# Large GpSimd operations of a two-layer hybrid decoder trunk move to VectorE and ScalarE

## The chip, the cores and the metric

The kernel runs on one core of a Trainium2 chip. The metric is the device time of one execution in microseconds: 1724.83 us, the median of 3 runs (1724.72 to 1726.2). The core has TensorE (matrix products, with a separate path that loads weights), VectorE, ScalarE and GpSimd (elementwise work and reductions), and SyncE, which issues the DMA transfers of this kernel. Each engine works through its own instructions in the order in which they were written out, and waits on semaphores for those of others.

## The reference

Sequence 512, width 1024, batch 1, two layers, all in float32. Each layer has three sub-layers with a pre-RMSNorm and a residual add:

```python
for l in range(DEPTH):
    h = rms_norm(x, norm_mix[l])
    p_a, p_b, p_c, p_d = jnp.split(h @ w_in[l], splits, axis=-1)
    y = jnp.concatenate([rglru_group(p_a, ...), retention_group(p_b, ...),
                         rwkv7_group(p_c, ...), ssd_group(p_d, ...)], axis=-1)
    x = x + y @ w_out[l]
    x = x + memory_cross_attention(rms_norm(x, norm_mem_q[l]), rms_norm(mem, norm_mem_kv[l]), ...)
    x = x + swiglu(rms_norm(x, norm_ffn[l]), ffn_w_in[l], ffn_w_out[l])
return rms_norm(x, norm_final)
```

The four mixer groups are 256 wide each. RG-LRU is a gated linear recurrence behind a causal convolution. Retention is decay attention in chunks of 128, followed by a norm over each head of 64 and a SiLU gate. RWKV-7 is a recurrence with a rank-one correction per step, followed by a head norm, a bonus term and a gate. The Mamba-2 SSD group is decay attention in chunks, followed by a gate and a group norm. Cross-attention has 4 heads over 256 memory tokens, and the FFN is 2816 wide.

## The kernel before

Activations lie transposed, as tiles of 128 channels by 512 tokens (kind `s`). Large products are taken in three parts for precision: a float32 operand is split into a high part, which ScalarE rounds to fp32r by a cast, and a low part, the source minus the high part, which is a subtraction. `mm3` (line 623) then runs high x high, high x low and low x high. `split_to` (line 600) splits activations. `weights` (line 608) loads a 128-column strip of a weight matrix by DMA into a tile `u`, casts it to a tile `v` on ScalarE and writes the low part, 128x1024, to a tile `w`. There are three tiles of each kind. `project` (line 633) multiplies all 8 tiles of the normalised input by such a strip into an accumulator of kind `a`.

The order of all instructions is not written by hand. Every call such as `V.tensor_tensor(...)` is recorded (`record`, line 291) with a modelled duration (`cost`, line 365: by engine and by elements, each engine by itself), and `order` (line 402) plans the whole program as a list: at each step it takes the operation that can start first, with a class and the longest path behind it as tie-breakers, and gives it its buffers. Weight loads have a class of their own that comes first at equal start, and dense projections keep their order among themselves and fill what is left. What the plan fixes is the order on each engine. Actual times come from the chip.

A layer runs as follows (`mix`, line 1317). `normed` (line 712) sums the squares of the 8 tiles, takes the reciprocal root in small steps on VectorE (`rsqrt`, line 561), and for each tile scales it by gain and norm and splits it. TensorE is given the projection of the memory tokens to K (`MemKV.k`, line 1604) to work on meanwhile. In layer 0 `mem_stats` (line 1362) sums the squares of the memory tokens. Then come the RWKV-7 projections and `rwkv_pair`, and `rwkv_solve` (line 1163), which inverts unit triangular 32x32 blocks on GpSimd in 62 small dependent operations, two per step, with a round trip through DRAM scratch on either side. Meanwhile TensorE has the projections of the SSD group, retention and RG-LRU. `rwkv_scan` (line 1233), `ssd` (line 814), `retention` (line 987) and `lru` (line 916) follow, then the head norms (`head_norm`, line 971) and the gates with their own projections, and at the end of the mixer V of the memory (`MemKV.v`, line 1630). The output projection, cross-attention and FFN come after.

Before the change GpSimd had, besides the solve:

- the low parts of the memory's K weights (layer 0: the strips 5 to 7 of 8; layer 1: all 8), of the gates' projections (`late`, line 1350: seven strips in each layer) and of the first half of the memory's V weights (four in each layer): 33 in all
- the low parts of every second tile in `normed`
- both elementwise passes of retention's head norm on each of its two tiles
- the products in `lru` (four in each layer), `lru_gate` and `ret_gate` (two each), and the additions of the state term in `ssd` (two in each of three chunks)
- the squares of the memory tokens and their sum in `mem_stats`
- the clearing of 16 tiles of 128x512 in `rwkv_solve` and `rwkv_scan`, beside that of the solve's own tile

Of the kernel before, what the change touches and what calls it, by code (L numbers as in the profile page):

```python
# [10 lines left out]
F32 = mybir.dt.float32  # L11
# [7 lines left out]
T = 512  # L19
L = 2  # L20
P = 128
# [496 lines left out]
class Trunk:  # L518
# [74 lines left out]

    def split(self, src, scale=None, n=T, eng=None):

        hi, lo = self.S(F32R), self.S(F32R)
        self.split_to(hi[:, :n], lo[:, :n], src, scale, eng)
        return hi, lo

    def split_to(self, hi, lo, src, scale=None, eng=None):  # L600
        if scale is None:
            self.A.copy(hi, src)
            (eng or self.V).tensor_tensor(lo, src, hi.bitcast(F32), op=ALU.subtract)
        else:
            self.A.activation(hi, src, AF.Copy, scale=scale)
            self.V.scalar_tensor_tensor(lo, src, scale, hi.bitcast(F32), op0=ALU.mult, op1=ALU.subtract)

    def weights(self, src, kt, cols, eng=None, parts=1, between=lambda: None):

        r, h, lo = [self.s.tile(k, dt)[:, :kt * cols].rearrange("p (k c) -> p k c", k=kt)  # L610
                    for k, dt in (("u", F32), ("v", F32R), ("w", F32R))]
        with self.s.mode(0, "w"):
            n = kt // parts
            for i in range(parts):
                ks = slice(i * n, (i + 1) * n)
                self.Q.dma_start(r[:, ks], src[i * n * P:(i + 1) * n * P].rearrange("(k p) c -> p k c", p=P))
                if i == 0:
                    between()
                self.A.copy(h[:, ks], r[:, ks])
                (eng or self.V).tensor_tensor(lo[:, ks], r[:, ks], h[:, ks].bitcast(F32), op=ALU.subtract)  # L620
        return h, lo
# [10 lines left out]

    def project(self, w_dram, c0, xs, eng=None):

        nk = len(xs)
        out = self.acc()
        for u0 in range(0, nk, 8):
            kt = min(8, nk - u0)
            h, lo = self.weights(w_dram[u0 * P:(u0 + kt) * P, c0:c0 + P], kt, P, eng)
# [72 lines left out]
    def normed(self, xs, gain):  # L712

        _, rb = self.rms(xs)
        hat = []
        for j, x in enumerate(xs):
            y = self.S()
            self.V.scalar_tensor_tensor(y, x, gain(j), rb, op0=ALU.mult, op1=ALU.mult)
            hat.append(self.split(y, eng=self.G if j % 2 else None))
        return hat  # L720
# [93 lines left out]
    def ssd(self, l, proj, dtcum):  # L814
# [11 lines left out]
        for j in range(4):  # L826
# [50 lines left out]
            for g in range(2):  # L877
                V.scalar_tensor_tensor(yy[g][:, tk], xs[g][:, tk], self.d["dh", l][:, g:g + 1], yb[:, g * P:(g + 1) * P],
                                       op0=ALU.mult, op1=ALU.add)
                if j:  # L880
                    G.tensor_tensor(yy[g][:, tk], yy[g][:, tk], yi[:, g], op=ALU.add)
            if j < 3:
# [33 lines left out]
    def lru(self, l, proj):  # L916
# [6 lines left out]
        for i in range(2):  # L923
# [22 lines left out]
            V.scalar_tensor_tensor(ti, ti, 1.0, xc, op0=ALU.add, op1=ALU.mult)  # L946
            G.tensor_tensor(ti, ti, rc, op=ALU.mult)
            res.append((a, ti, t))
        for y, (a, ti, t) in zip(yy, res):

            self.s.link(last, A.activation(t, t, AF.Sqrt), True)
            G.tensor_tensor(ti, ti, t, op=ALU.mult)
            V.tensor_tensor_scan(y, a, ti, 0.0, op0=ALU.mult, op1=ALU.add)
        return yy

    def lru_gate(self, l, proj, yy):
        V, A = self.V, self.A
        res = []
        for i in range(2):
# [6 lines left out]
            V.scalar_tensor_tensor(q, q, 1.0, x, op0=ALU.add, op1=ALU.mult)  # L966
            self.G.tensor_tensor(yy[i], q, yy[i], op=ALU.mult)
            res.append((yy[i], 0.5))
        return res

    def head_norm(self, y, eps, eng):

# [6 lines left out]
        V.tensor_scalar(m[:, :n], m[:, :n], 1.0 / HD, None, op0=ALU.mult)  # L979
        eng.tensor_tensor(y3, y3, over(m), op=ALU.subtract)  # L980
        sq = self.S()
        A.activation(sq, y, AF.Square)
        V.tensor_reduce(m[:, n:], sq.rearrange("p (g c) -> p g c", c=HD), axis=AX.X, op=ALU.add)
        V.tensor_scalar(m[:, n:], m[:, n:], 1.0 / HD, eps, op0=ALU.mult, op1=ALU.add)
        eng.tensor_tensor(y3, y3, over(self.rsqrt(m[:, n:], n)), op=ALU.mult)

    def retention(self, l, proj, vals):
# [62 lines left out]
        for t in yt:  # L1050
            self.head_norm(t, 1e-5, G)
        yy = []
# [8 lines left out]
    def ret_gate(self, l, proj, yy):  # L1061
        res = []
        for i in range(2):
            g = self.two_silu(proj(COL_B + 768 + i * P))
            self.G.tensor_tensor(yy[i], yy[i], g, op=ALU.mult)
            res.append((yy[i], 0.5))
        return res
# [95 lines left out]
    def rwkv_solve(self, l, nd):  # L1163


        A, G = self.A, self.G
        B, H = 32, 16
# [23 lines left out]
        for k, f in enumerate((rt, rf)):  # L1191
# [4 lines left out]
            for i in range(2):  # L1196
                t = self.S()
                self.s.link(done, G.memset(t, 0.0), False)
                t3 = t.rearrange("p (n x) -> p n x", n=8)
# [33 lines left out]
    def rwkv_scan(self, l, pairs, RT):  # L1233


        V, A, E, G = self.V, self.A, self.E, self.G
        ident = self.con("ident")
# [55 lines left out]
        for i in range(2):  # L1293
            y = yt[i]
            self.head_norm(y, HD * 1e-5, V)
            b = self.bank()
# [20 lines left out]
    def mix(self, l, xs, kv):  # L1317
# [30 lines left out]
        with part("lru"):  # L1348
            ya = self.lru(l, proj)
        late = lambda c0: self.project(w, c0, hat, self.G)  # L1350
        with part("rwkv_gate"):
            rc = self.rwkv_gate(l, lora, late, yc)
        with part("ssd"):
            rd = self.ssd_gate(l, late, yd)
        with part("ret"):
            rb = self.ret_gate(l, late, yb)
        with part("lru"):
            ra = self.lru_gate(l, late, ya)
        kv.v(0)
        return ra + rb + rc + rd  # L1360

    def mem_stats(self, xs):

        V, A, E, G = self.V, self.A, self.E, self.G
# [206 lines left out]
class MemKV:  # L1571


    def weights(self, d, **k):
        tr = self.tr
        early = self.l == 0
        return tr.weights(tr.a["mem_wk"][self.l][:, d * P:(d + 1) * P], KD, P, tr.V if early and d in (0, 1, 2, 3, 4) else tr.G,
                          2 if early and d < 3 else 1, **k)

# [50 lines left out]
    def v(self, dh):  # L1630
# [36 lines left out]
```

## Time and profile before

| | |
|---|---|
| median of 3 runs | 1724.83 us (1724.72 to 1726.2) |
| the profiled execution: its own time | 1725.3 us |
| the profiled execution: span from first to last instruction | 1723.5 us |
| TensorE products | 96% of the span |
| VectorE | 1017.1 us, 59% |
| ScalarE | 631.1 us, 37% |
| GpSimd | 220.1 us, 13% |
| mean granted clock of TensorE | 0.985 of full speed |

Nearly all instructions carry one line of the source, 515, where the planned order is issued. So groups are told apart by tile names: `a` and `b` are accumulators, `s` activations, `t` small columns, `u`, `v`, `w` weights with their high and low parts, `n` the solve's matrix, `cst` and `prm` constants and parameters. In the rows PE is TensorE, DVE VectorE, ACT ScalarE, POOL GpSimd and SP SyncE. `fp32r` after a form marks a high or a low part. A group's mean is in nanoseconds, and all else is in microseconds from the first instruction.

### The profile page before, as it was taken

What the parts mean: (1) busy time and instruction counts of PE and PEld (TensorE: products, weight loads), DVE (VectorE), ACT (ScalarE), POOL (GpSimd) and SP (SyncE); (2) the same over time, 40 slices, a digit from 0 to 9 for tenths busy, and PEclk for the clock granted to TensorE, in tenths of its full rate; (3) what the DMA queues carried; (4) which work ended last, traced back from release to release, by engine and by line L of the source; (5) the groups of instructions that cost most, each with busy time, mean ns of one, the idle gap of its engine ahead of it and who ended that gap; (6) DMA issues with size and microseconds to landing.
All of it is one profiled execution on the core that took longest, in us unless ns stands there. A gap on an engine that the chain in (4) does not pass through costs nothing.

```text
span 1723.5 us, 21453 instructions
## 1 busy us (share of the span) xinstructions
PE 1662.0 (96%) x8344; PEld 1354.3 (79%) x8344; DVE 1017.1 (59%) x1700; ACT 631.1 (37%) x962; POOL 220.1 (13%) x240
## 2 busy tenths in 40 slices
PE   7898998999999999999989989999999999999997
PEld 6686776888788888888887867778887888888886
DVE  7766668675665554432467656876665645554323
ACT  6434234444442332222345333454443422332221
POOL 2316025300000000000050421351000000000001
PEclk9998999999999999999999999999999999999999
DMA  7434121441333333333453341116322333233331
GB/s 232 124 100 109 39 55 52 150 141 55 92 98 97 89 96 98 95 98 106 142 163 87 99 92 52 47 61 190 92 79 88 91 98 98 87 97 92 95 95 62
DMA packets 312901, 169.49 MB, mean 98 GB/s; under 512 B 35936, under 2 KB 300384, under 8 KB 312672
## 3 DMA queue, kind: packets, MB, share of 16 engines
q1 hardware_dynamic: 312800, 168.12, 34.1%
q8 instruction: 66, 1.08, 0.3%
q14 instruction: 35, 0.29, 0.1%
HBM read 156.56 MB, written 9.44 MB: 96 GB/s over the span
## 4 chain that ended last, share of the span: by engine, by line
PE 82%; DVE 6%; POOL 3%; ACT 1%; issue 1%; DMA 1%; SPq 1%; DVEq 0%; POOLq 0%; ACTq 0%
PE a L515 73%; PE b L515 10%; DVE s L515 4%; DVE t L515 2%; POOL s L515 2%; POOL n L515 2%; ACT s L515 1%; SPq L515 1%; ACT v L515 0%; DVE w L515 0%; DMA s<-fd 0%; DMA n<-nd 0%; DMA s<-in_lora_dram 0%; DMA nd<-s 0%; DVEq L1663 0%
## 5 line engine op out<-in xcount | busy, mean ns | idle before, releaser
L515 PE MATMUL a<-s,v 128*128 128x512 f32 (+1 forms) x4012 | 1242.5, 389 | 14.5 <-ACT s L515 8.9
L515 PEld LDWEIGHTS a<-s,v 128*128 128x128 f32 x4012 | 748.9, 190 | 174.5 <-ACT s L515 9.7
L515 PE MATMUL a<-s,w 128*128 128x512 f32 (+1 forms) x2006 | 781.9, 390 | 2.8 <-POOL w L515 1.7
L515 ACT CAST v<-u 128x1024 fp32r<-128x1024 f32 (+3 forms) x275 | 282.2, 1027 | 681.1 <-PE a L515 380.7
L515 PEld LDWEIGHTS a<-s,w 128*128 128x128 f32 x2006 | 381.5, 190 | 83.7 <-POOL w L515 1.9
L515 DVE TENSOR_TENSOR w<-u,v 128x1024 fp32r<-128x1024 f32 (+3 forms) x242 | 293.1, 1212 | 154.3 <-ACT v L515 150.9
L515 DVE TENSOR_TENSOR s<-a,s 128x512 f32<-128x512 f32 (+1 forms) x132 | 90.7, 691 | 260.9 <-PE a L515 242.2
L515 ACT ACTIVATE s<-s 128x512 f32<-128x512 f32 (+3 forms) x229 | 142.1, 628 | 123.9 <-DVE s L515 110.1
L515 PE MATMUL b<-s,s 128*64 128x64 f32 (+8 forms) x1268 | 151.3, 273 | 17.3 <-DVE s L515 6.1
L515 POOL TENSOR_TENSOR w<-u,v 128x1024 fp32r<-128x1024 f32 x33 | 82.6, 2507 | 640.7 <-ACT v L515 609.1
L515 PEld LDWEIGHTS b<-s,s 128*128 128x128 f32 (+3 forms) x1268 | 122.1, 167 | 53.0 <-issue 16.0
L515 DVE TENSOR_TENSOR s<-s,s 128x512 f32<-128x512 f32 (+3 forms) x184 | 133.8, 733 | 27.4 <-ACT s L515 21.4
L515 POOL TENSOR_TENSOR s<-s,s 128x512 f32<-128x512 f32 (+3 forms) x45 | 54.7, 1229 | 688.3 <-ACT s L515 561.4
L515 DVE SCALAR_TENSOR_TENSOR s<-s,s 128x512 f32<-128x512 f32 (+2 forms) x164 | 115.9, 711 | 23.4 <-ACT s L515 22.8
L515 DVE TENSOR_TENSOR s<-s,a 128x512 f32<-128x512 f32 (+1 forms) x49 | 33.2, 677 | 100.9 <-PE a L515 100.9
L515 DVE SCALAR_TENSOR_TENSOR s<-s,prm,s 128x512 fp32r<-128x512 f32 (+3 forms) x78 | 63.1, 833 | 8.8 <-ACT s L515 8.5
L515 PE MATMUL a<-v,s 128*128 128x260 f32 (+1 forms) x256 | 66.7, 343 | 0.0
L515 ACT COPY s<-b 64x256 f32<-64x256 f32 (+3 forms) x92 | 30.5, 353 | 98.2 <-PE b L515 96.5
L515 PE MATMUL b<-cst,s 128*128 128x128 f32 (+2 forms) x312 | 52.4, 281 | 6.8 <-POOL s L515 3.2
L515 PEld LDWEIGHTS b<-cst,s 128*128 128x128 f32 x312 | 41.7, 172 | 15.4 <-POOL s L515 4.1
L515 ACT CAST s<-s 128x512 fp32r<-128x512 f32 x48 | 29.5, 620 | 62.1 <-DVE s L515 57.0
L515 DVE SCALAR_TENSOR_TENSOR s<-a,prm,s 128x511 f32<-128x511 f32 (+2 forms) x64 | 47.6, 744 | 2.0 <-ACT s L515 1.2
(94 smaller groups left out, 788.5 us busy)
## 6 DMA issues: line engine op xcount, KB each, us to landing
u<-in_ffn_w_in_dram SPq DMA_DIRECT2D x88, 512.0 KB, 3.7
u<-in_w_in_dram SPq DMA_DIRECT2D x52, 512.0 KB, 3.8
u<-in_ffn_w_out_dram SPq DMA_DIRECT2D x32, 512.0 KB, 3.7
u<-in_mem_wv_dram SPq DMA_DIRECT2D x16, 512.0 KB, 3.6
u<-in_w_out_dram SPq DMA_DIRECT2D x16, 512.0 KB, 3.9
u<-in_mem_wq_dram SPq DMA_DIRECT2D x16, 512.0 KB, 3.8
u<-in_mem_wo_dram SPq DMA_DIRECT2D x16, 512.0 KB, 3.7
u<-in_mem_wk_dram SPq DMA_DIRECT2D x13, 512.0 KB, 3.8
```

Of the source, the lines that this page charges most:

```text
L515: op.fn(*[real(x) for x in op.args], **{k: real(x) for k, x in op.kw.items()})
```

## The change

All of the operations listed above leave GpSimd. The squares of `mem_stats` go to ScalarE, the rest to VectorE. GpSimd keeps the solve with the clearing of its own tile, and three scalings in `finish` (line 1522), each taken in two halves. The parameters that named an engine go. Nothing else is edited, but the plan is worked out again from the new list, so the order on every engine may differ. The core of the diff:

```diff
-    def split_to(self, hi, lo, src, scale=None, eng=None):
+    def split_to(self, hi, lo, src, scale=None):
-            (eng or self.V).tensor_tensor(lo, src, hi.bitcast(F32), op=ALU.subtract)
+            self.V.tensor_tensor(lo, src, hi.bitcast(F32), op=ALU.subtract)
...
-                (eng or self.V).tensor_tensor(lo[:, ks], r[:, ks], h[:, ks].bitcast(F32), op=ALU.subtract)
+                self.V.tensor_tensor(lo[:, ks], r[:, ks], h[:, ks].bitcast(F32), op=ALU.subtract)
...
-            hat.append(self.split(y, eng=self.G if j % 2 else None))
+            hat.append(self.split(y))
...
-                    G.tensor_tensor(yy[g][:, tk], yy[g][:, tk], yi[:, g], op=ALU.add)
+                    V.tensor_tensor(yy[g][:, tk], yy[g][:, tk], yi[:, g], op=ALU.add)
...
-            G.tensor_tensor(ti, ti, rc, op=ALU.mult)
+            V.tensor_tensor(ti, ti, rc, op=ALU.mult)
...
-            G.tensor_tensor(ti, ti, t, op=ALU.mult)
+            V.tensor_tensor(ti, ti, t, op=ALU.mult)
...
-        eng.tensor_tensor(y3, y3, over(m), op=ALU.subtract)
+        V.tensor_tensor(y3, y3, over(m), op=ALU.subtract)
...
-        eng.tensor_tensor(y3, y3, over(self.rsqrt(m[:, n:], n)), op=ALU.mult)
+        V.tensor_tensor(y3, y3, over(self.rsqrt(m[:, n:], n)), op=ALU.mult)
...
-                self.s.link(done, G.memset(t, 0.0), False)
+                self.s.link(done, V.memset(t, 0.0), False)
...
-                self.s.link(self.solved, G.memset(t, 0.0), False)
+                self.s.link(self.solved, V.memset(t, 0.0), False)
...
-        late = lambda c0: self.project(w, c0, hat, self.G)
-            rc = self.rwkv_gate(l, lora, late, yc)
+            rc = self.rwkv_gate(l, lora, proj, yc)
...
-            self.s.link(self.s.anchor, G.tensor_tensor(sq, m, m, op=ALU.mult), False)
+            self.s.link(self.s.anchor, A.activation(sq, m, AF.Square), False)
...
-                G.tensor_tensor(s, s, sq, op=ALU.add)
+                V.tensor_tensor(s, s, sq, op=ALU.add)
...
-            h, wl = tr.weights(tr.a["mem_wv"][self.l][u * 256:(u + 1) * 256, dh * T:(dh + 1) * T], 2, T, None if dh else tr.G)
+            h, wl = tr.weights(tr.a["mem_wv"][self.l][u * 256:(u + 1) * 256, dh * T:(dh + 1) * T], 2, T)
```

In this order the edits are in `split_to`, `weights`, `normed`, `ssd`, `lru` (two), `head_norm` (two), `rwkv_solve`, `rwkv_scan`, `mix`, `mem_stats` (two) and `MemKV.v`. `MemKV.weights` loses its choice of engine in the same way, and the three other gates are called with `proj` too. One product each in `lru_gate` and `ret_gate` moves likewise. `link(a, b, False)` puts `b` behind `a` in the plan. It adds no semaphore of its own.

## Rows read from the trace of the kernel before

**Rows 1.** The page: busy time by engine (1), one costly group (5).

```profile
PE 1662.0 (96%) x8344; PEld 1354.3 (79%) x8344; DVE 1017.1 (59%) x1700; ACT 631.1 (37%) x962; POOL 220.1 (13%) x240
...
L515 ACT ACTIVATE s<-s 128x512 f32<-128x512 f32 (+3 forms) x229 | 142.1, 628 | 123.9 <-DVE s L515 110.1
```

**Rows 2.** Busy time by stretch: span, each engine (x instructions), PEclk, DMA share, GB/s.

```profile
23.00:62.00 39.00, 28.87 (x156) 23.94 (x157) 32.89 (x32) 15.75 (x24) 26.32 (x17) 0.87 0.57 171
246.00:288.00 42.00, 34.74 (x169) 27.11 (x170) 38.21 (x99) 20.90 (x31) 19.16 (x11) 0.94 0.12 38
866.00:899.00 33.00, 27.44 (x208) 26.40 (x207) 27.35 (x28) 16.08 (x27) 23.17 (x13) 0.95 0.54 158
155.00:172.00 17.00, 11.08 (x67) 8.57 (x66) 8.69 (x17) 8.97 (x18) 4.22 (x11) 0.70 0.64 122
```

**Rows 3.** TensorE's timeline: start, length, instruction, [idle before, what ended it].

```profile
49.97 0.50 PE L515 MATMUL a<-s,v 128*128 128x512 f32 x1 [4.05 <-DVE s L515]
...
273.16 0.66 PE L515 MATMUL b<-cst,s 128*128 128x128 f32 x4 [1.58 <-POOL s L515]
...
282.24 0.82 PE L515 MATMUL b<-s,s 128*128 128x512 f32 x2 [2.88 <-DVE s L515]
```

**Rows 4.** Timeline of GpSimd and VectorE, lengths in us.

```profile
256.50 3.03 POOL L515 TENSOR_TENSOR w<-u,v 128x1024 fp32r<-128x1024 f32 x1 [5.18 <-ACT v L515]
...
257.18 2.38 DVE L515 TENSOR_SCALAR t<-t 128x8 f32<-128x8 f32 x1
...
887.99 0.68 DVE L515 TENSOR_TENSOR s<-s,s 128x512 fp32r<-128x512 f32 x1
```

**Rows 5.** VectorE by form, 866 to 899 us: count, busy us, mean ns, idle.

```profile
L515 DVE SCALAR_TENSOR_TENSOR s<-s,prm,s 128x512 f32<-128x512 f32 x8 | 11.2, 1453 | 1.6 <-ACT s L515 1.6
...
L515 DVE TENSOR_TENSOR s<-s,s 128x512 fp32r<-128x512 f32 x4 | 6.4, 1598 | 1.2 <-ACT s L515 1.2
...
L515 DVE TENSOR_TENSOR w<-u,v 128x1024 fp32r<-128x1024 f32 x2 | 4.5, 2294 | 0.0
...
L515 DVE TENSOR_TENSOR s<-s,s 128x512 f32<-128x512 f32 x1 | 2.5, 2509 | 0.7 <-ACT s L515 0.7
...
L515 DVE SCALAR_TENSOR_TENSOR t<-t,t 128x4 f32<-128x4 f32 x6 | 1.0, 164 | 0.2
```

**Rows 6.** VectorE by form, 23 to 62 us.

```profile
L515 DVE SCALAR_TENSOR_TENSOR s<-s,prm,s 128x512 f32<-128x512 f32 x8 | 10.6, 1366 | 1.8 <-ACT s L515 1.8
...
L515 DVE TENSOR_TENSOR s<-s,s 128x512 fp32r<-128x512 f32 x6 | 9.0, 1508 | 1.4 <-ACT s L515 1.4
...
L515 DVE SCALAR_TENSOR_TENSOR t<-t,t 128x4 f32<-128x4 f32 x6 | 3.1, 524 | 0.2
...
L515 DVE TENSOR_SCALAR t<-t 128x4 int32<-128x4 int32 x2 | 2.3, 1166 | 0.1
```

**Rows 7.** VectorE by form, 62 to 121 us.

```profile
L515 DVE TENSOR_TENSOR w<-u,v 128x1024 fp32r<-128x1024 f32 x5 | 6.1, 1226 | 3.3 <-ACT v L515 2.9 <-issue 0.2
...
L515 DVE SCALAR_TENSOR_TENSOR s<-s,prm,s 128x512 f32<-128x512 f32 x2 | 1.5, 752 | 0.1
```

**Rows 8.** VectorE by form, 246 to 288 us.

```profile
L515 DVE SCALAR_TENSOR_TENSOR t<-t,t 128x8 f32<-128x8 f32 x24 | 8.1, 366 | 0.1
...
L515 DVE TENSOR_SCALAR t<-t 128x8 f32<-128x8 f32 x7 | 4.1, 600 | 0.0
...
L515 DVE TENSOR_TENSOR s<-s,s 128x512 f32<-128x512 f32 x2 | 2.4, 1208 | 2.8 <-ACT s L515 2.8
```

**Rows 9.** GpSimd by form, 246 to 288 us.

```profile
L515 POOL TENSOR_TENSOR w<-u,v 128x1024 fp32r<-128x1024 f32 x3 | 7.8, 2606 | 7.7 <-ACT v L515 5.2 <-PE b L515 2.5
...
L515 POOL TENSOR_TENSOR s<-s,t 128x512 f32<-128x512 f32 x4 | 5.3, 1314 | 13.7 <-DVE t L515 13.7
```

**Rows 10.** Chain of waits, 304 to 376 us: start, length, what.

```profile
304.77 70.10 PE a L515 x302
```

**Rows 11.** VectorE's waits by releaser: us in total, times, longest us.

```profile
DVE w L515 <- ACT v L515: 150.9, 141, 4.8
```

More of the change, by code (lines that the diff above doesn't have):

```diff
@@ L592, in softplus, with split @@
         V.scalar_tensor_tensor(out, h, 2.0, s, op0=ALU.mult, op1=ALU.add)
-    def split(self, src, scale=None, n=T, eng=None):
+    def split(self, src, scale=None, n=T):
         hi, lo = self.S(F32R), self.S(F32R)
-        self.split_to(hi[:, :n], lo[:, :n], src, scale, eng)
+        self.split_to(hi[:, :n], lo[:, :n], src, scale)
         return hi, lo
-    def split_to(self, hi, lo, src, scale=None, eng=None):
+    def split_to(self, hi, lo, src, scale=None):
         if scale is None:
             self.A.copy(hi, src)
-            (eng or self.V).tensor_tensor(lo, src, hi.bitcast(F32), op=ALU.subtract)
+            self.V.tensor_tensor(lo, src, hi.bitcast(F32), op=ALU.subtract)
         else:
@@ L606, in split_to, with weights @@
             self.V.scalar_tensor_tensor(lo, src, scale, hi.bitcast(F32), op0=ALU.mult, op1=ALU.subtract)
-    def weights(self, src, kt, cols, eng=None, parts=1, between=lambda: None):
+    def weights(self, src, kt, cols, parts=1, between=lambda: None):
         r, h, lo = [self.s.tile(k, dt)[:, :kt * cols].rearrange("p (k c) -> p k c", k=kt)
@@ L631, in dense, with project @@
         return self.s.mode(2, "d")
-    def project(self, w_dram, c0, xs, eng=None):
+    def project(self, w_dram, c0, xs):
         nk = len(xs)
@@ L638, in project @@
             kt = min(8, nk - u0)
-            h, lo = self.weights(w_dram[u0 * P:(u0 + kt) * P, c0:c0 + P], kt, P, eng)
+            h, lo = self.weights(w_dram[u0 * P:(u0 + kt) * P, c0:c0 + P], kt, P)
             with self.dense():
@@ L966, in lru_gate, with head_norm @@
             V.scalar_tensor_tensor(q, q, 1.0, x, op0=ALU.add, op1=ALU.mult)
-            self.G.tensor_tensor(yy[i], q, yy[i], op=ALU.mult)
+            V.tensor_tensor(yy[i], q, yy[i], op=ALU.mult)
             res.append((yy[i], 0.5))
         return res
-    def head_norm(self, y, eps, eng):
+    def head_norm(self, y, eps):
         V, A = self.V, self.A
@@ L1050, in retention @@
         for t in yt:
-            self.head_norm(t, 1e-5, G)
+            self.head_norm(t, 1e-5)
         yy = []
@@ L1064, in ret_gate @@
             g = self.two_silu(proj(COL_B + 768 + i * P))
-            self.G.tensor_tensor(yy[i], yy[i], g, op=ALU.mult)
+            self.V.tensor_tensor(yy[i], yy[i], g, op=ALU.mult)
             res.append((yy[i], 0.5))
@@ L1163, in rwkv_solve @@
     def rwkv_solve(self, l, nd):
-        A, G = self.A, self.G
+        V, A, G = self.V, self.A, self.G
         B, H = 32, 16
@@ L1233, in rwkv_scan @@
     def rwkv_scan(self, l, pairs, RT):
-        V, A, E, G = self.V, self.A, self.E, self.G
+        V, A, E = self.V, self.A, self.E
         ident = self.con("ident")
@@ L1294, in rwkv_scan @@
             y = yt[i]
-            self.head_norm(y, HD * 1e-5, V)
+            self.head_norm(y, HD * 1e-5)
             b = self.bank()
@@ L1349, in mix @@
             ya = self.lru(l, proj)
-        late = lambda c0: self.project(w, c0, hat, self.G)
         with part("rwkv_gate"):
-            rc = self.rwkv_gate(l, lora, late, yc)
+            rc = self.rwkv_gate(l, lora, proj, yc)
         with part("ssd"):
-            rd = self.ssd_gate(l, late, yd)
+            rd = self.ssd_gate(l, proj, yd)
         with part("ret"):
-            rb = self.ret_gate(l, late, yb)
+            rb = self.ret_gate(l, proj, yb)
         with part("lru"):
-            ra = self.lru_gate(l, late, ya)
+            ra = self.lru_gate(l, proj, ya)
         kv.v(0)
@@ L1362, in mem_stats @@
     def mem_stats(self, xs):
-        V, A, E, G = self.V, self.A, self.E, self.G
+        V, A, E = self.V, self.A, self.E
         s = None
@@ L1576, in weights @@
         early = self.l == 0
-        return tr.weights(tr.a["mem_wk"][self.l][:, d * P:(d + 1) * P], KD, P, tr.V if early and d in (0, 1, 2, 3, 4) else tr.G,
-                          2 if early and d < 3 else 1, **k)
+        return tr.weights(tr.a["mem_wk"][self.l][:, d * P:(d + 1) * P], KD, P, 2 if early and d < 3 else 1, **k)
     def load(self, i):
```

## The prediction

> **What bounds the kernel now.** I read the page first. TensorE is busy 1662.0 us of the span of 1723.5 us, and no other engine is near that; GpSimd, whose work the change takes away, is busy 220.1 us [rows 1]. So the kernel can win only where TensorE stands (61.5 us in all) or where its granted clock falls, and VectorE can be loaded further without harm wherever TensorE stays busy. The next view is therefore the busy time of each engine in the few stretches in which TensorE stands [rows 2]. The reader should compare the first column with the width of each stretch, and then look at VectorE, GpSimd and PEclk.
>
> - The normalisation at the head of layer 0, 23 to 62 us: TensorE is busy 28.87 of 39 us, VectorE 32.89, GpSimd 26.32, and the mean granted clock is 0.87 of full speed (the clock has two levels, 2.4 and 1.2 GHz, so it ran at the lower one for about a quarter of the stretch).
> - The same place in layer 1, 866 to 899 us: 27.44 of 33 us for TensorE, 27.35 for VectorE, 23.17 for GpSimd, clock 0.95.
> - The end of the token mixer, 246 to 288 us, where head norms, RG-LRU and gates finish: TensorE 34.74 of 42 us, VectorE 38.21, clock 0.94. Layer 1 repeats it 844 us later, at 1090 to 1132.
> - The end of the triangular solve, 155 to 172 us: TensorE 11.08 of 17 us, but VectorE only 8.69. Layer 1 repeats it too.
>
> In the first three, VectorE is nearly full; in the fourth it is not. The third view, TensorE's timeline with what ended each wait, says the same: before 49.97 us it stood 4.05 us for a product of VectorE, before 273.16 us 1.58 us for one of GpSimd, before 282.24 us 2.88 us for one of VectorE [rows 3].
>
> The fourth view is why VectorE is full. At 257.18 us a VectorE operation on 128x8 elements took 2.38 us, and it ended with the 3.03 us GpSimd operation that had begun at 256.50 [rows 4]. The same kind of small operation takes 0.164 us where nothing is in its way [rows 5]. So VectorE operations stand inside their own busy time while a large GpSimd operation runs. The means per form show how often: the scaling by gain and norm, 128x512, averages 1.366 us in the first stretch and 1.453 us in layer 1 [rows 5, 6], against 0.752 us between 62 and 121 us, where GpSimd is idle [rows 7].
>
> **The change, part by part.** All prices are those of VectorE alone: a low part of 128x1024 weights 1.226 us [rows 7], a pass of 128x512 with two operands 0.68 us [rows 4].
>
> *Head of layer 0.* What VectorE loses to GpSimd now: 8 x (1.366 - 0.752) = 4.9 us in the scalings, 6 x (1.508 - 0.68) = 5.0 us in the subtractions of the splits, 6 x (0.524 - 0.164) = 2.2 us and 2 x (1.166 - 0.164) = 2.0 us in the small steps of the reciprocal root, 14.1 us together [rows 4 to 7]. What it takes over: three low parts of the memory's K weights, 3.7 us, and the low parts of four of the eight normalised tiles, 2.7 us, so 6.4 us. Net -7.7 us on the queue for which TensorE waits. The three additions of the memory's squares, 2.1 us, come over as well; they are needed only much later, and if the plan puts them before the last tile the net is -5.6. I take -7. The four squares go to ScalarE at 0.628 us each, 2.5 us [rows 1]; ScalarE is busy 15.75 of these 39 us [rows 2], which hides them; without that cover they cost the 2.5 us. Clock: 0.13 of 39 us is 5.1 us; if the long stands shrink, some of it returns. I take -2, bounds 0 and -5. The floor: TensorE stands 10.1 us here.
>
> *Head of layer 1.* Lost now: 8 x (1.453 - 0.752) = 5.6, 4 x (1.598 - 0.68) = 3.7, 2 x (2.294 - 1.226) = 2.1, and 2.509 - 0.68 = 1.8 in the last addition ahead of the sum of squares, 13.2 us [rows 4, 5, 7]. Taken over: six of the eight K low parts start after 866 us, 7.4 us, and four tiles, 2.7 us: 10.1 us. Net -3.1. I take -3, and -1 of the 0.05 x 33 = 1.7 us of clock. The bounds are 0 (the low parts come in front of the scalings) and the 5.6 us that TensorE stands plus the 1.7.
>
> *End of the mixer, in each layer.* Lost now: 24 x (0.366 - 0.164) = 4.8, 7 x (0.600 - 0.164) = 3.1, 2 x (1.208 - 0.68) = 1.1 us, together 9.0 [rows 4, 5, 8]. Taken over: three low parts, 3.7 us, four head-norm passes, 2.7 us, four products of RG-LRU, 2.7 us: 9.1 us [rows 4, 7, 9]. The queue as a whole wins nothing. But the head-norm passes lie in series with VectorE's reductions and the transposes, at 1.314 us each on GpSimd [rows 9]; at 0.68 four save 2.5 us, and the way to another engine and back is gone. I take -2 per layer, so -4, with bounds of -8 (all of TensorE's 7.3 us and some clock) and +4 (half of the 9.1 us lies in front of the chain without relief).
>
> *Where it costs nothing.* The other 16 of the 33 low parts, the gate products, and the additions of the SSD state lie beside TensorE at full work. Clearing 16 tiles beside the two solves has no VectorE row: between nothing and the 0.68 us pass, at most 5.4 us per layer. I take the upper end, since it is the nearest row of that width. VectorE has 8.3 us free in 155 to 172 us, and that hides it; were it not hidden, the tile that the solve's result lands in would be late by up to 5.4 us. The solve itself stays on GpSimd, and so does the wait of TensorE at its end: 0, with +-3 for a plan that feeds TensorE a little more or less ahead of it. No DMA is moved; GpSimd's queue loses work and nobody gets behind it.
>
> *New waits.* A low part waits for ScalarE's cast of the same weights. On GpSimd nothing was queued behind it; on VectorE the scalings, reductions and roots are, and TensorE waits for those.
>
> Sum: -7 - 2 - 3 - 1 - 4 = -17 us. The profiled execution took 1725.3 us, 0.5 us above the median of 1724.83, so I forecast 1725.3 - 17 = 1708.3, as a median 1708.
>
> The Trainium skill speaks against the change (Perfetto Trace Analysis, Optimizing Scalar/DVE Operations): where VectorE is saturated, giving work to ScalarE or even GpSimd may make sense, though it adds that the two engines' shared read port may spoil this. The trace bears out the second half: 9.0 us lost against 9.1 us taken over at the end of the mixer. By the first half alone that stretch would pay the 9.1 us in each layer, which is the second rival below. SBUF - State Buffer (Two separate sides) calls the shared pair an exclusive lock held for a whole instruction; the 2.38 us row agrees.
>
> **The rivals.**
> - *More comes back.* If VectorE's queue is no longer last, TensorE stands for almost nothing in the three stretches: -10.1 - 5.6 - 2 x 7.3 = -30 us without the clock, 1695. For it: the losses sum over stretches that each other feed. Against it: a normalised tile still costs 0.752 + 0.68 us of VectorE against three products of 0.232 us on TensorE (302 in 70.10 us) [rows 10], so TensorE starves at the head of a layer whatever GpSimd does.
> - *VectorE saturated.* The gates' low parts and products lie in front of the chain and the relief lands elsewhere: -13 for the heads, +2 x 9.1: 1725.3 + 5.2 = 1730.5. For it: 38.21 of 42 us busy. Against it: 9.0 us of those are waiting.
> - *Low parts block VectorE's queue* (slower). Seventeen low parts, 3 + 8 + 2 x 3, move into or just ahead of the tight stretches. VectorE waited 150.9 us for ScalarE's casts at 141 of its own, 1.07 us each, 4.8 us at the longest [rows 11]. If each of the 17 waits the mean with a chain behind it, 18 us go and the gain is gone: 1726.5; at 2 us each it is 1725.3 - 17 + 34 = 1742. It decides from 1.2 us each. Against it: before, the planner knew nothing of GpSimd's grip on VectorE, and without it its order fits the chip better.
> - *The plan moves.* Every engine's order is worked out anew from the same cost table. If one projection (24 products of 0.232 us, 5.6 us) lands on the wrong side of a stand, half of the gain is given back: about 1717, or the two ends cancel and nothing measurable is left, 1723.
>
> **How the numbers follow.** This kernel's measurement can tell about 0.2% (3.4 us) from no change, so faster is below 1721.4. The forecast, 1700 to 1720, has 0.54; more comes back 0.17; the plan moves 0.16, half of it still faster; VectorE saturated 0.05; blocked queue 0.08. Faster 0.79, same 0.08, slower 0.13. The range 1690 to 1722 leaves out the two slower cases and the far end of the first rival.
>
> **What would show it.** Right: GpSimd has only the solve, a few clears and the final scalings; the 128x512 scalings of the heads average near 0.75 us in both layers; the small steps at 246 to 288 us near 0.16 us; TensorE's stands at the head of layer 0 fall from 10.1 to about 4 us; the stand at the solve's end is what it was. VectorE's whole busy time hardly grows. Wrong: VectorE waiting for casts inside these stretches, or TensorE's stands at the end of the mixer above 7.3 us per layer, or a longer stand at the end of a solve.

## The result and the profile after

After the change the median is 1687.03 us (1686.89 to 1689.78, 4 runs) against 1725.51 us for the kernel before (4 runs): a ratio of 0.978, 95% interval 0.9763 to 0.9797. The gain is 38.5 us where 17 were forecast. The profiled execution took 1689.78 us, its span is 1688.0 us. The page of the kernel after, busy times and the chain that ended last by engine:

```profile
PE 1650.0 (98%) x8344; PEld 1348.4 (80%) x8344; DVE 1013.4 (60%) x1796; ACT 632.1 (37%) x966; POOL 67.5 (4%) x140
...
PE 89%; POOL 4%; DMA 3%; DVE 1%; SPq 1%; ACT 1%; issue 1%; DVEq 0%; POOLq 0%; ACTq 0%
```

Against [rows 1] GpSimd is down from 220.1 to 67.5 us, and VectorE did not grow: 1013.4 against 1017.1 us with 96 instructions more. What came over is about as long as the standing that went away. TensorE stands 1688.0 - 1650.0 = 38.0 us, before 61.5. The windows of the kernel after (columns as in rows 2) are the heads of the layers, the end of the mixer and the two ends of a solve:

```profile
20.00:58.00 38.00, 34.90 (x199) 29.00 (x199) 31.60 (x61) 24.23 (x41) 0.77 (x3) 0.91 0.68 202
227.00:269.00 42.00, 42.00 (x231) 33.56 (x230) 36.35 (x91) 20.57 (x33) 0.00 (x0) 1.00 0.18 51
849.00:881.00 32.00, 32.00 (x234) 30.16 (x233) 25.38 (x41) 18.56 (x30) 0.78 (x3) 1.00 0.69 200
138.00:164.00 26.00, 18.70 (x121) 14.33 (x120) 14.38 (x28) 9.49 (x19) 5.46 (x13) 0.80 0.53 108
965.00:992.00 27.00, 18.54 (x107) 14.31 (x107) 13.55 (x26) 9.42 (x18) 7.33 (x19) 0.75 0.52 110
```

The first three answer the first three of [rows 2]. At the end of the mixer and at the head of layer 1 TensorE is now busy all the time at the full clock: 42.00 of 42 us (34.74 before) and 32.00 of 32 (27.44 of 33 before); at the head of layer 0 it stands 3.1 us (10.1 before). The last two rows went the other way. The same places of the kernel before:

```profile
150.00:176.00 26.00, 20.08 (x151) 15.72 (x149) 12.77 (x25) 9.60 (x19) 8.20 (x24) 0.80 0.61 132
994.00:1021.00 27.00, 21.42 (x181) 16.74 (x181) 14.04 (x26) 10.11 (x20) 9.14 (x24) 0.87 0.60 127
```

TensorE is busy 18.54 instead of 21.42 us there in layer 1, at a granted clock of 0.75 instead of 0.87. Its timeline after shows one long wait in each layer for the result of the solve on its way through scratch memory; before it was 2.45 and 2.35 us behind a first wait of 3.48 and 3.23. First layer 0 before, then both layers after:

```profile
161.16 0.45 PE L515 MATMUL b<-cst,t 128*128 128x128 f32 x1 [3.48 <-ACT s L515]
...
164.49 0.44 PE L515 MATMUL b<-s,s 64*64 64x64 f32 x2 [2.45 <-DMA s<-fd]
```

```profile
153.61 0.44 PE L515 MATMUL b<-s,s 64*64 64x64 f32 x2 [7.30 <-DMA s<-fd]
...
982.55 0.44 PE L515 MATMUL b<-s,s 64*64 64x64 f32 x2 [8.46 <-DMA s<-fd]
```

VectorE by form, first between 20 and 50 us (three rows), then 227 to 269 us:

```profile
L515 DVE TENSOR_TENSOR w<-u,v 128x1024 fp32r<-128x1024 f32 x8 | 9.8, 1223 | 2.0 <-ACT v L515 2.0
L515 DVE SCALAR_TENSOR_TENSOR s<-s,prm,s 128x512 f32<-128x512 f32 x8 | 5.9, 745 | 0.8 <-ACT s L515 0.8
L515 DVE SCALAR_TENSOR_TENSOR t<-t,t 128x4 f32<-128x4 f32 x6 | 1.0, 160 | 0.2
...
L515 DVE TENSOR_SCALAR t<-t 128x8 f32<-128x8 f32 x8 | 1.2, 163 | 0.0
L515 DVE SCALAR_TENSOR_TENSOR t<-t,t 128x8 f32<-128x8 f32 x6 | 0.9, 158 | 0.0
L515 DVE TENSOR_TENSOR s<-s,t 128x512 f32<-128x512 f32 x4 | 2.7, 684 | 0.0
```

The scaling takes 745 ns where [rows 6] had 1366, the small steps 158 to 163 ns where [rows 6, 8] had 366 to 600, and the head-norm pass 684 ns on VectorE where [rows 9] had 1314 on GpSimd.

Where the 35.5 us of span came from, by the start of the same operation in both timelines:

| from, to | before (us) | after (us) | gained by then | in this stretch |
|---|---|---|---|---|
| first operation of the solve, layer 0 | 121.99 | 108.99 | 13.0 | 13.0 |
| first product on its result | 164.49 | 153.61 | 10.9 | -2.1 |
| first load of `mem_wq` (end of mixer) | 344.98 | 326.74 | 18.2 | 7.4 |
| first operation of the solve, layer 1 | 966.55 | 938.82 | 27.7 | 9.5 |
| first product on its result | 1009.13 | 982.55 | 26.6 | -1.2 |
| first load of `mem_wq` | 1188.88 | 1153.81 | 35.1 | 8.5 |
| end | 1723.53 | 1688.00 | 35.5 | 0.5 |

The kernel after, profiled once more in `after_again`, reaches the same places up to 3.0 us earlier (the first load of `mem_wq` at 323.73), so single lines are good to 2 or 3 us.

### The profile page after: what moved, and what is told of

It reads as the page before. It is cut to its first block, busy times and chain, and to the rows that moved or that the text cites. A ratio compares the mean times of both kernels' runs of the same rounds, so it can differ in the third digit from the quotient of the medians.

```text
span 1688.0 us, 21391 instructions
## 1 busy us (share of the span) xinstructions
PE 1650.0 (98%) x8344; PEld 1348.4 (80%) x8344; DVE 1013.4 (60%) x1796; ACT 632.1 (37%) x966; POOL 67.5 (4%) x140
## 4 chain that ended last, share of the span: by engine, by line
PE 89%; POOL 4%; DMA 3%; DVE 1%; SPq 1%; ACT 1%; issue 1%; DVEq 0%; POOLq 0%; ACTq 0%
PE a L515 79%; PE b L515 10%; POOL s L515 2%; POOL n L515 2%; DVE s L515 1%; SPq L515 1%; DMA s<-s 1%; ACT s L515 1%; DMA fd<-s 0%; DMA s<-fd 0%; DMA nd<-s 0%; DMA n<-nd 0%; DMA s<-in_memT_dram 0%; ACT v L515 0%; DVE w L515 0%
## 5 line engine op out<-in xcount | busy, mean ns | idle before, releaser
L515 DVE TENSOR_TENSOR w<-u,v 128x1024 fp32r<-128x1024 f32 (+3 forms) x275 | 329.5, 1199 | 171.2 <-ACT v L515 170.6
L515 PE MATMUL b<-s,s 64*64 64x64 f32 (+8 forms) x1268 | 149.5, 272 | 16.7 <-DMA s<-fd 15.8
L515 DVE TENSOR_TENSOR s<-s,s 128x512 f32<-128x512 f32 (+4 forms) x223 | 140.2, 636 | 16.5 <-ACT s L515 9.2
L515 DVE SCALAR_TENSOR_TENSOR s<-s,s 128x512 f32<-128x512 f32 (+2 forms) x164 | 110.5, 677 | 9.4 <-ACT s L515 9.0
L515 ACT COPY s<-b 64x256 f32<-64x256 f32 (+3 forms) x92 | 30.1, 354 | 90.4 <-PE b L515 81.6
L515 DVE SCALAR_TENSOR_TENSOR s<-s,prm,s 128x512 fp32r<-128x512 f32 (+3 forms) x78 | 52.8, 695 | 4.5 <-ACT s L515 4.4
L515 PEld LDWEIGHTS a<-v,s 128*128 128x128 f32 x256 | 43.7, 188 | 5.7
L515 PE MATMUL a<-w,s 128*128 128x512 f32 (+1 forms) x128 | 43.9, 343 | 0.0
```

The source lines that it names most:

```text
L515: op.fn(*[real(x) for x in op.args], **{k: real(x) for k, x in op.kw.items()})
```

## The experiments

**Engine against order.** The change does two things at once: it moves work, and every engine's order is planned anew with other prices. Two kernels take them apart by giving an operation the account and price of one engine in the plan and the instruction to another.

`oldplan_vector`, the order of before, the work on VectorE (the squares too):

```diff
+        self.GX = Engine(self.s, "POOL", self.nc.vector)
-            hat.append(self.split(y, eng=self.G if j % 2 else None))
+            hat.append(self.split(y, eng=self.GX if j % 2 else None))
...
```

> The order of every engine is planned as in the kernel before (the moved operations still priced as GpSimd's), but they are issued to VectorE at the places that the plan gave them; the squares of the memory go to VectorE too. Theory A, GpSimd's large operations make VectorE stand: the plan doesn't matter, 1690 us (1680 to 1700). Theory B, the gain is the newly worked-out order: 1720 to 1727 us. Theory C, GpSimd's results simply come late (slow operations and the way between engines): 1690 us as well; the echo runs tell A from C.

`newplan_gpsimd`, the order of after, the work on GpSimd (the squares stay on ScalarE):

```diff
+        self.GX = Engine(self.s, "DVE", self.nc.gpsimd)
-            hat.append(self.split(y))
+            hat.append(self.split(y, eng=self.GX if j % 2 else None))
...
```

> The reverse: the order of the changed kernel, planned as if VectorE did all of it, but the moved operations (not the squares, which stay on ScalarE) are issued to GpSimd. Theory A and theory C: the gain is gone, 1720 to 1745 us, and VectorE's 128x512 scalings at the heads are above 1.2 us again. Theory B: 1685 to 1695 us.

Measured: 1704.25 us, 0.9867 [0.9849, 0.9886], and 1709.52 us, 0.9896 [0.9875, 0.9916]. Both lie outside every range that had been expected. So the engine is worth 21.3 us in the old order (1725.5 to 1704.25) and 22.5 in the new one (1709.5 to 1687.0), and the order 16.0 and 17.2 (with the move of the squares to ScalarE, which is taken apart below): the two nearly add up, and neither alone is the gain. The prediction had only the first.

**Is it the reading of GpSimd that VectorE stands for?** Two kernels leave the kernel after as it is and give GpSimd unused work behind each of the 41 moved low parts, whose results nobody uses. `echo_read` subtracts the low part from itself, 384 columns at a time; `echo_clear` reads one column and then only clears.

```diff
+                if op.low:
+                    for c in range(0, _free(lo), 384):
+                        part = rows[:, c:min(c + 384, _free(lo))]
+                        gp.tensor_tensor(junk[:, :_free(part)], part, part, op=ALU.subtract)
```

> The changed kernel with all its work on VectorE; beside it, behind each of the 41 low parts that moved, GpSimd subtracts that low part from itself into a scratch tile that nobody reads, 384 columns at a time. Nobody waits for GpSimd here. Theory A: VectorE stands again, and of the 38 us some half comes back: 1705 us (1697 to 1718), with the scalings at the heads above 1.0 us. Theory C: nobody needs the results, so 1687 us (1684 to 1691), and the scalings stay at 0.75 us.

```diff
+                if op.low:
+                    gp.tensor_tensor(junk[:, 0:1], one, one, op=ALU.subtract)
+                    for _ in range(6 if _free(lo) == KD * P else 4):
+                        gp.memset(junk, 0.0)
```

> As echo_read, but GpSimd only writes: behind each of the 41 low parts one column is subtracted, and then the scratch tile is cleared six times (four behind the 512-wide ones), which keeps GpSimd busy about as long. If any GpSimd operation stops VectorE (theory A1): as echo_read, about 1705 us. If only one that reads SBUF stops operations of VectorE with two operands there (theory A2): 1687 to 1692 us. Theory C: 1687 us.

Measured: `echo_read` 1714.65 us, 0.9929 [0.9913, 0.9945]; `echo_clear` 1690.98 us, 0.9796 [0.9775, 0.9817]. GpSimd is equally busy in both, 184.4 and 180.7 us on their pages. VectorE by form between 20 and 62 us, `echo_read` and then `echo_clear`:

```profile
L518 DVE TENSOR_TENSOR w<-u,v 128x1024 fp32r<-128x1024 f32 x8 | 11.0, 1370 | 0.5 <-ACT v L518 0.5
L518 DVE SCALAR_TENSOR_TENSOR s<-s,prm,s 128x512 f32<-128x512 f32 x8 | 7.8, 988 | 0.0
L518 DVE SCALAR_TENSOR_TENSOR t<-t,t 128x4 f32<-128x4 f32 x6 | 2.3, 385 | 0.2
```

```profile
L518 DVE TENSOR_TENSOR w<-u,v 128x1024 fp32r<-128x1024 f32 x9 | 11.0, 1224 | 2.6 <-ACT v L518 2.3 <-POOL junk L522 0.3
L518 DVE SCALAR_TENSOR_TENSOR s<-s,prm,s 128x512 f32<-128x512 f32 x8 | 5.9, 744 | 0.8 <-ACT s L518 0.8
L518 DVE SCALAR_TENSOR_TENSOR t<-t,t 128x4 f32<-128x4 f32 x6 | 1.0, 161 | 0.2
```

Reading costs 27.6 us though nobody uses what GpSimd writes; the scaling rises from 745 to 988 ns and the small step from 160 to 385. VectorE waited for GpSimd to let go of a tile for 1.5 us in all, in either run, so that does not tell them apart. Clearing for the same time leaves these three forms as they were (744, 161, 1224 ns) and costs 4.0 us. The Trainium skill (SBUF - State Buffer, Two separate sides) says that a VectorE operation with two inputs in that memory is held up only by a GpSimd operation that reads there; both rows agree. So the wait is inside VectorE's busy time, for these forms, all with two inputs, it comes from GpSimd's reads, and it is shown, not argued.

It is not so for every form. Operations with one tile as input, `TENSOR_SCALAR`, did stand for the clears. The two most affected forms over the whole run, in the kernel after and then in `echo_clear`, and one case in `echo_clear`:

```profile
L515 DVE TENSOR_SCALAR s<-s 128x512 f32<-128x512 f32 x18 | 7.4, 419 | 2.6 <-ACT s L515 2.6
L515 DVE TENSOR_SCALAR t<-t 128x8 int32<-128x8 int32 x28 | 4.6, 164 | 0.3
```

```profile
L518 DVE TENSOR_SCALAR s<-s 128x512 f32<-128x512 f32 x18 | 8.8, 495 | 2.6 <-ACT s L518 2.6
L518 DVE TENSOR_SCALAR t<-t 128x8 int32<-128x8 int32 x28 | 6.9, 247 | 0.3
```

```profile
260.82 1.92 POOL L524 MEMSET junk<- 128x384 f32 x4
...
262.32 0.45 DVE L518 TENSOR_SCALAR t<-t 128x8 int32<-128x8 int32 x1
```

The fourth clear ends at 262.74 and the small operation at 262.77. These two forms are 3.7 us longer in all. That the 4.0 us of `echo_clear` come from there was not tested.

**Which place.** Both kernels have the order of after. `heads_on_gpsimd` gives GpSimd the low parts of every second normalised tile, of the memory's K weights, and the memory's additions; `mixer_on_gpsimd` all the others.

```diff
-            hat.append(self.split(y, eng=self.GX if j % 2 else None))
+            hat.append(self.split(y, eng=self.V if j % 2 else None))
...
-            self.head_norm(t, 1e-5, self.V)
+            self.head_norm(t, 1e-5, self.GX)
...
-        late = lambda c0: self.project(w, c0, hat, self.V)
+        late = lambda c0: self.project(w, c0, hat, self.GX)
```

(from the first to the second)

> The order of the changed kernel, but what moved at the two heads of a layer (low parts of the memory's K, of every second normalised tile, additions of the memory's squares) is issued to GpSimd again. By the prediction's terms the heads are worth 13 us, so 1700 us; by the two traces, in which the solves start 13.0 and another 9.3 us earlier, 22 us, so 1709 us (1703 to 1716).

> The order of the changed kernel, but what moved in the mixer (low parts of the gates' projections and of V, head-norm passes, products of RG-LRU and the gates, additions of the SSD state, clears) is issued to GpSimd again. By the prediction's terms it is worth 4 us, so 1691 us; by the two traces, in which the way from the end of a solve to the output projection is 8.2 and 9.0 us shorter, 17 us, so 1704 us (1698 to 1712).

Measured: 1697.92 us, 0.9831 [0.9803, 0.986], and 1702.62 us, 0.9857 [0.9828, 0.9885]. The heads are worth 10.9 us and the mixer 15.6 us, together 26.5 against 22.5 for both at once. The kernel after itself gave 1687.03 and, on another chip, 1688.39 us, so each is good to about 1.5 us. The mixer, forecast at 4 us, is the larger of the two.

**What is in the order.** `lock_plan` is the kernel before, with the planner told that large reading operations of GpSimd and all of VectorE's exclude each other, and that GpSimd goes first where both could start at once.

```diff
+                    if e == "POOL" and self.large(op):
+                        t = max(t, clock["DVE"])
...
+            if e == "POOL" and self.large(op):
+                clock["DVE"] = max(clock["DVE"], end)
```

> The kernel before with every operation on the engine that had it; only the planner is told that a large GpSimd operation that reads (256 columns or more) and any VectorE operation exclude each other. Before, it let the two run beside each other in its own account. The question is what the 16 to 17 us are that the new order alone gave back (newplan_gpsimd, oldplan_vector). Theory P (the old order cost that much because the planner filled VectorE and GpSimd at the same time, which the chip can't do): an order that knows it wins most of them with no work moved, 1705 to 1715. Theory Q (the new order is better because GpSimd's slower prices and its separate queue are gone from the plan, and knowledge of the exclusion alone doesn't give that back): 1720 to 1727, or slower, since an order that lets GpSimd hold VectorE on purpose plans more stands for TensorE (its own account ends at 1598 instead of 1532 us).

Measured: 1744.9 us, 1.0098 [1.0079, 1.0118]. Theory P falls for this planner: VectorE's busy time fell to 987.0 us, 30.1 less than before for the same operations, so it did stand less, but the plan kept it idle for that, and TensorE stood 1743.6 - 1672.1 = 71.5 us by its page. Two more kernels separate the squares, which `newplan_gpsimd` had left on ScalarE:

```diff
+        self.GA = Engine(self.s, "ACT", self.nc.gpsimd)
-            self.s.link(self.s.anchor, A.activation(sq, m, AF.Square), False)
+            self.s.link(self.s.anchor, self.GA.tensor_tensor(sq, m, m, op=ALU.mult), False)
```

> newplan_gpsimd (the order of the kernel after, the large operations on GpSimd) with the four squares of the memory tokens on GpSimd too, as in the kernel before; their place in the order is that of the kernel after. newplan_gpsimd had them on ScalarE, so the 16 us that are put down to the order hold this move as well. Theory S (the squares are a good part of the 16 us: 4 x 1.48 us of GpSimd at the head of layer 0, in which VectorE stands): the solve of layer 0 starts 4 to 6 us later and the time is 1713 to 1716. Theory O (it is the order itself): 1709 to 1711.

```diff
-            self.s.link(self.s.anchor, G.tensor_tensor(sq, m, m, op=ALU.mult), False)
+            self.s.link(self.s.anchor, A.activation(sq, m, AF.Square), False)
```

> The kernel before with one edit: the four squares of the memory tokens go from GpSimd to ScalarE, and the order is planned anew. Theory S: the solve of layer 0 starts 4 to 8 us earlier, 1717 to 1721. Theory O: the squares are worth 0 to 3 us, 1722 to 1725.

Measured: `newplan_squares` 1714.37 us, 0.993 [0.9904, 0.9956], the solve of layer 0 at 115.93 us instead of 111.7 in `newplan_gpsimd`. The intervals of the two overlap, so the 4.9 us are not clear of noise, but 4.2 us of them lie at the place expected. What is left, 1725.8 - 1714.4 = 11.4 us (8 to 17 by its interval), is order alone, with every operation on the engine that had it before. The traces show where it lies: by the operations of the table `newplan_squares` is 6.1 us ahead of the kernel before at the solve of layer 0 and wins another 5.3 between the first load of `mem_wq` and the solve of layer 1; all other stretches together give 1.8 (the profiled execution is 1.8 us faster than the median). So the order won its time in the two stretches that hold the heads of the layers. VectorE also stands less in it: it is busy 1006.7 instead of 1017.1 us with the same 1700 instructions. The largest difference is in small steps of the head norms, before and in `newplan_squares`:

```profile
L515 DVE TENSOR_SCALAR t<-t 128x8 f32<-128x8 f32 x16 | 8.6, 545 | 0.0
```

```profile
L515 DVE TENSOR_SCALAR t<-t 128x8 f32<-128x8 f32 x16 | 2.3, 162 | 0.0
```

14 of these 16 were in the two stretches of [rows 8] and its like in layer 1, at the end of the mixer, so they do not explain what was won at the heads. `squares_only` took 1724.56 us, 0.9988 [0.9974, 1.0002]: its solve starts 7.7 us earlier, at 114.31 us, but the first load of `mem_wq` comes at 345.21 us against 344.98. Planned anew, the solve and the mixer gave all of it back. So an edit's gain at one place is not kept unless the plan behind it keeps it; which decision of the new order is worth the 11.4 us was not found.

**The stands that came up at the solves.** In the kernel after, TensorE's largest stands are 7.30 and 8.46 us, each followed by a stretch at the lower of the two clocks (granted clock 0.50 from 153.6 to 158.0 and from 982.5 to 991.0 us). The planner prices an operation of the solve and the copy through scratch memory too low: in its own account the solve takes about 27 us, on the chip it took 144.41 - 108.99 = 35.4 us, so too little work lies beside it. `fit_solve` raises both prices:

```diff
-            op.lat = 1700.0 + op.bytes / 350.0
+            op.lat = (2600.0 if any(r.root.kind == "d" for r in ins + [out] if isinstance(r, Ref)) else 1700.0) + op.bytes / 350.0
...
-            op.dur = rate * n + (60 if fn != "tensor_tensor" else 110)
+            op.dur = rate * n + (60 if fn != "tensor_tensor" else 240)
```

> The changed kernel, with the planner's prices for the solve's operations (130 ns more each) and for transfers through DRAM scratch (0.9 us more) nearer to the trace, where the solve takes 35.4 us against 27.2 planned and TensorE then stands 7.3 and 8.5 us. If TensorE stands there because the plan puts too little work ahead of the solve's result: 10 to 20 us faster than the changed kernel, 1667 to 1677 us, with the stands at the solves below 3 us. If the filler is only borrowed from the end of the mixer, where the plan now shows stands of 5.7 us per layer: 1680 to 1688 us.

`fit_solve_pe` also prices each product at 18 instead of 4 ns above its columns:

> As fit_solve, and the planner's price of a product 18 ns instead of 4 ns above its columns, since products of 512 columns follow each other every 0.232 us in the trace. The plan then has no stands in the mixer at all. If the plan's prices are what keeps TensorE standing: at or below fit_solve, 1660 to 1675 us. If the gain of fit_solve came from somewhere else: 1680 to 1690 us.

Measured: 1684.86 us, 0.9753 [0.972, 0.9786], and 1686.7 us, 0.9767 [0.9738, 0.9796]. The stands at the solves nearly go, and new ones come at the end of the mixer: the work was borrowed from there. Then half of the raise (170 instead of 240, 2200 instead of 2600) with the scalings of `finish` on VectorE, the full raise with the same `finish`, and the kernel after on the same chip:

```diff
-                        G.tensor_tensor(t[:, k], xg[j + k][:, ts], rb, op=ALU.mult)
+                        V.tensor_tensor(t[:, k], xg[j + k][:, ts], rb, op=ALU.mult)
```

> The kernel after, with the planner's price of an operation of the solve raised by 60 ns and of a copy through the scratch memory by 0.5 us (about half of what fit_solve raised), and with the last three scalings of finish on VectorE. Theory B (what is laid beside the solve is only borrowed from the end of the mixer): the stand behind each solve falls to 4 to 5 us, a smaller one appears at the end of the mixer, the total is within 2 us of fit_solve; with 0.5 us less at the end of the kernel 1682 to 1685. Theory A (half as much filler is free): both stands fall, 1678 to 1681.

> fit_solve with the last three scalings of GpSimd, those in finish, on VectorE. They are the last large GpSimd operations beside VectorE's scalings of the same place. If the standing holds there too, VectorE's 128x256 scalings fall from 0.78 to about 0.41 us and the end of the kernel comes 0.5 to 1 us earlier: 1684 against 1684.9. If the end hangs on the sum of squares and on TensorE, not on these scalings, 1684.9 is kept.

> The kernel after, on the same chip as the two variants of it: 1687 us, ratio 0.978 against the kernel before; by it fit_finish and fit_half_finish are told to within 1 us.

Measured: `fit_half_finish` 1674.33 us, 0.9694 [0.9678, 0.971]; `fit_finish` 1685.29 us, 0.9757 [0.9739, 0.9774]; the kernel after 1688.39 us, 0.9775 [0.9758, 0.9791]. `finish` is worth nothing that can be measured (1685.29 against 1684.86), and half of the raise is worth 14.1 us, more than either theory said. The ends of the solves in `after_again` and in `fit_half_finish`, and then the product on the result in layer 0 of the latter:

```profile
138.00:164.00 26.00, 18.63 (x172) 14.32 (x170) 14.84 (x32) 9.41 (x19) 4.66 (x12) 0.87 0.52 102
965.00:992.00 27.00, 18.17 (x136) 14.00 (x134) 13.41 (x29) 8.06 (x17) 4.70 (x14) 0.75 0.49 98
```

```profile
138.00:164.00 26.00, 22.26 (x190) 17.43 (x188) 17.80 (x35) 11.16 (x21) 4.58 (x12) 0.93 0.65 132
965.00:992.00 27.00, 22.71 (x217) 16.93 (x216) 15.40 (x32) 9.15 (x21) 0.00 (x0) 0.94 0.54 108
```

```profile
152.10 0.29 PE L515 MATMUL b<-s,s 64*64 64x64 f32 x2 [3.38 <-DMA s<-fd]
```

The stand is 3.38 instead of 7.37 us, and the granted clock 0.93 and 0.94 instead of 0.87 and 0.75: clock alone is (0.06 x 26) + (0.19 x 27) = 6.7 us, the stands at the solves are 16.2 - 7.7 = 8.5 us shorter (in layer 1 there are two, 1.98 and 2.31). Together that is 15.2 us and covers the 14.1. In `fit_finish` two stands are at the end of the mixer:

```profile
300.35 0.66 PE L515 MATMUL b<-cst,s 128*128 128x128 f32 x4 [2.32 <-DVE s L515]
...
303.05 1.52 PE L515 MATMUL a<-s,v 128*128 128x512 f32 x2 [2.04 <-ACT s L515]
```

A quarter (140, 1950) and three quarters (200, 2400) tell whether the half was luck:

> fit_half_finish with a quarter of what fit_solve raised: 30 ns for each operation of the solve and 0.25 us for a copy through the scratch memory. If the gain of fit_half_finish over the kernel after (14 us) is the stand behind the solve, and the lower clock that follows on a long stand, it is monotonous here: stands of 5 to 6 us behind each solve, still followed by the lower clock, 1680 to 1684. If fit_half_finish was one lucky order among many, the time may land anywhere between 1674 and 1690, without the stand telling which.

> fit_half_finish with three quarters of what fit_solve raised: 90 ns and 0.7 us. If more work beside the solve is taken from the end of the mixer, stands behind the solve of 2 to 3 us and first stands at the end of the mixer: 1676 to 1682. If there is work enough, both small: 1671 to 1674.

Measured: 1680.75 us, 0.9736 [0.9711, 0.9761], and 1684.31 us, 0.976 [0.9732, 0.9787]. From none to a quarter to a half the time falls, 1688.4, 1680.8, 1674.3, with the stands at the solves, 16.2, 11.7, 7.7 us, as the first reading says. At three quarters these stands fall on to 5.5 us, stands of 1.1 us begin at the end of each mixer, and the time is 10 us longer, outside both ranges expected. Those 2.2 us don't explain it. TensorE's busy time is 1652.1 us against 1642.2 of the half, and lower clock (0.993 against 0.995, about 3 us) is a part of that; the rest was not located, so that the optimum lies at just this half may be luck. `fit_half_finish` is the fastest version found.

## Why the prediction missed its size

Two steps failed. The sum has no term for the new order, which gave 11.4 us by itself. And the end of the mixer went in at 4 us, where the work was worth about 8 in the old order and 15.6 in the new one. In the order that the prediction had before it, the work moved was worth 21.3 us (`oldplan_vector`) against the 17 forecast: by the operations of the table 14.4 at the heads, where 13 were forecast, and 8.1 between the solves' results and the loads of `mem_wq`, where 4 were.

- *What bounds the kernel, and the price of standing: right.* Stands and clock carried the result: 61.5 to 38.0 us of stands, and (1 - 0.985) x 1723.5 - (1 - 0.989) x 1688.0 = 7.3 us of clock, 30.8 of the 35.5 us of span. About 5 us lie inside TensorE's busy time, unexplained. The forms fell to the unhindered prices, and VectorE's busy time did not grow.
- *The heads: right in size for the work.* Forecast 13 us. With the order of after the work itself is worth 10.9 us and the squares, whose removal from GpSimd the sum held at the head, about 4.9. The two stretches that end at a solve gained 13.0 + 9.5 = 22.5 us in the table; half of that is the order. In layer 0 the stands fell from 10.1 to 3.1 us; about 4 was forecast.
- *The end of the mixer: mis-sized.* "The queue as a whole wins nothing", so -2 per layer, bounds -8 to +4. Measured 15.6 us for everything that moved in both mixers, or 7.4 and 8.5 us in the table, at the far bound. The sum of queue time (9.0 lost, 9.1 taken over) was the wrong measure: VectorE is still 36.35 us busy there, yet TensorE no longer stands. The time given back was in the steps of the head norms and roots, 366 and 600 ns before and 158 and 163 after, which depend on one another; that what came over lies beside this chain fits the rows but was not shown. Why the same work is worth more in the new order than in the old one stays open. *More comes back* (1695, chance 0.17) had the outcome, TensorE standing for almost nothing there, and its time was still 8 us too long.
- *The order: put at nothing.* The plan was a rival that could only lose 9 to 15 us (1717 and 1723 against 1708). It gained 11.4 us with every engine unchanged, although its own account got longer (1536.0 instead of 1532.0 us). That the new order fits better stood in the prediction as half a sentence and got no price.
- *The solve: "0, with +-3", and an unchanged stand.* The stands grew in both layers, from 5.9 to 7.3 and from 5.6 to 8.5 us, and the clock in layer 1 fell. The stretches lost 2.1 and 1.2 us, inside the bound, but a longer stand was named as a sign of being wrong. The loss hid under the gain; half a correction of two prices won 14 us there, more than the change had lost.
- *Low parts in front of VectorE's chain: didn't happen.* VectorE's wait for casts grew from 150.9 [rows 11] to 170.6 us. Of the 170.6, 10.4 us lie between 834 and 870 us at the head of layer 1, where TensorE is busy throughout:

```profile
DVE w L515 <- ACT v L515: 170.6, 160, 4.8
```

- *Clears: the upper end was near.* Two clears of 128x512 on VectorE took 1.03 us, for which 0.68 each was taken:

```profile
139.06 1.03 DVE L515 MEMSET s<- 128x512 f32 x2
```

The sum as measured: heads 10.9, squares 4.9, mixer 15.6, less 4.0 that the two places share, order 11.4, together 38.8 us; the runs gave 38.5. The terms are differences along one row of kernels, from before to after, so they must add up to about the gain; that they do is no test of the single terms.

## What to carry to other kernels

Read the busy time of an engine by form against the same form where nothing hinders it: what lies above may be a wait that no view shows as one, and time can come back even if as much work is added to the same engine. When an edit makes a planner lay everything out anew, measure the new order with the old engines and the old order with the new engines; here the order was 11 to 16 us of 38. After a gain, look for the stand that has grown: here it was a transfer through scratch memory that the planner priced too low, and of what half a correction won there 6.7 us were clock and 8.5 the stand itself.

## What had not been expected of the hardware

GpSimd clearing memory for 97.6 us beside VectorE cost VectorE's operations on two tiles nothing (744 and 1224 ns), while its reads raised the same forms to 988 and 1370 ns. `TENSOR_SCALAR`, with one tile as input, did stand for the clears: 247 instead of 164 ns. And the solve on GpSimd, whose work did not change, took 35.4 us instead of 33.7 in layer 0: one of its two kinds of subtraction is longer by 36 ns each, 2.2 us over both layers. It goes with the new order and not with a busier VectorE: with VectorE's added work in the old order (`oldplan_vector`) that solve takes 33.9 us, and in the new order without that work on VectorE (`newplan_gpsimd`) 35.5. What in the order does it stays open. Here the rows of GpSimd, before and after:

```profile
L515 POOL TENSOR_TENSOR n<-n,s 128x126 f32<-128x126 f32 (+22 forms) x62 | 27.8, 448 | 136.9 <-DMA n<-nd 132.2
```

```profile
L515 POOL TENSOR_TENSOR n<-n,s 128x126 f32<-128x126 f32 (+22 forms) x62 | 30.0, 484 | 134.2 <-DMA n<-nd 129.5
```
